# Adding transfers of a gated attention and gMLP block, moved from the vs stage and the first u pair to the pairs of keys, values and queries

## Chip, cores and metric

The kernel runs on one core of a Trainium2 chip, in one launch. The metric is the device time of an execution in microseconds (us). An engine is named as in the profile: PE (TensorE matmuls), DVE (VectorE), ACT (ScalarE), POOL (GpSimd) and SP (SyncE). POOL and SP each feed a DMA queue; ACT's is hardly used.

## What is computed

One layer over 1024 positions of width 1024, in float32. All weights of the input projection are one matrix `w_in`, whose columns are split among q, k, v, za, u, vs, zs and the merge gates.

```python
h = rmsnorm(x, norm_g[l])
q, k, v, za, u, vs, zs, gm = jnp.split(h @ w_in[l], IN_SPLITS, axis=-1)
q, k = partial_rope(q), partial_rope(k)
a = window_sink_attention(q, k, v, att_sinks[l])
a = (a * silu(za)) @ w_att_out[l]
sgo = chunked_spatial_gating(gelu(u), gelu(vs), sg_w[l], sg_b[l], sg_ln_g[l], sg_ln_b[l])
sgo = (sgo * silu(zs)) @ w_sg_out[l]
ga, gs = jnp.split(sigmoid(gm + b_merge[l]), 2, axis=-1)
x = x + (ga * a + gs * sgo) @ w_o[l]
return rmsnorm(x, final_g)
```

`chunked_spatial_gating` normalises vs over its 1024 columns and mixes it over 128 positions with a masked matrix of each channel group; the result is multiplied by u.

## The kernel before

**Split products.** Every float32 factor is split into a high and a low part of TensorE's rounded float32 type: ACT casts the high part, DVE subtracts it for the low one (`split`, lines 188 and 189). A product then takes three matmuls (high by high, high by low, low by high).

**Pairs and seven products.** The large products are made a pair of 128-column blocks of weights at a time (`gemm_pair`), by Strassen's scheme (in Winograd's form): seven products of 128 by 512 by 512 in place of eight. One product is 12 matmuls of 128x512 (`product`, line 399). The scheme needs four sums of each weight pair's quarters. For some pairs (u, keys and values, q and others: `pair_job`) DVE makes them from the loaded tiles `wr` (lines 291 to 295); the first sum needs the second loaded tile of the pair, r1. For the others (`early_job`) they are made in DRAM, long before their use, by **adding transfers**: six DMA steps for each pair, which POOL issues (line 351): two plain copies (512 KB each) and four transfers that add 256 KB to what is there. The list `early` holds 88 steps: six steps each of twelve pairs of weights, and 16 of `w_o` (line 534). They are taken from the front of the list, one at a time, by `part_of_early`, which is called at hooks in the program. Outside the attention stage 44 steps at most may be taken (`keep_of_early`); the rest go beside attention.

**Pacing.** A step is not free to go as soon as POOL reaches it: `paced` makes it wait for the instruction in `pace[0]`. While `by_products[0]` is set, that is a matmul in the middle of the latest product (`product`, at k equal to 1), otherwise a copy by ACT (`mark`). POOL takes its instructions in order, so everything behind a step in POOL's order waits too.

**Stages.** In order: the norm of x; the vs stage (`vs_gemm`, `plain`, `take`), written out by hand in its order; four pairs of u; one pair of keys and values; four pairs of q; two of zs; then attention beside eight pairs of gates, in a written order; then the rest of zs, za, the two output projections, `w_o` and the last norm. Outside the written parts a scheduler at build time sets each engine's order; the order of PE's instructions in all of these pairs is that of the code.

**A pair in time.** In `gemm_pair` ACT copies the first product out of its PSUM bank (x11, line 433), negates the second (x22, line 440) and copies the third's sum (x12, line 443), and DVE adds the later products to these (lines 448, 455, 459). The third product goes on into the bank that x11 is copied from, so that it can't begin before that copy. Four times in a pair `split_next` splits a tile of weights for what comes next; the loads of the pair after next start when its three buffers `wr` come free. A hook is called seven times in a pair, after each product's part.

In the u pairs the hook also mixes: PE multiplies the normalised vs by the mixing matrix into a bank `ps_tp` (line 1126), of which there are two; DVE scales it (line 1134) and multiplies u by it (line 1142), which frees the bank; SP stores the result. Ahead of the first mixing DVE normalises vs (line 1090).

In the pair of keys and values POOL issues the stores of k (`k_dr`, line 1189) and, after a transposition, of v (`v_dr`, line 1204). Their tiles lie in a pool that the q stage's tiles reuse: the first tiles `qhl` (line 1256 on ACT) and `rot` (line 1276 on POOL, and the load of the rotary tables by SP, line 1231) wait until all those stores have landed. A q pair writes each of its four results as a split tile `qhl` (three buffers), which SP stores (`q_hl`, line 1261).

Of the kernel before, what the change touches and what calls it, by code (L numbers as in the profile page):

```python
# [54 lines left out]
def hybrid_tile(  # L55
# [40 lines left out]
    def bank(tag, dt=F32):  # L96
        return pools.get(tag, psum).tile([P, 512], dt, name=nm("ps_" + tag), tag="ps_" + tag, bufs=2)
# [10 lines left out]
    def xtile():  # L108
        return mtile([P, HALF], F32, "x", 5)
# [98 lines left out]
    def new_b(names=FORMS):  # L208
        return {n: (slot(n + "h"), slot(n + "l")) for n in names}
# [38 lines left out]
    def split_next(hold=False):  # L248

        if not units:  # L250
            begin_job()
        if not units:
            return
        halves, keys = units.pop(0)
        if keys[0][1] == 2 and not locked[0]:
            make_sums(behind_of.get(keys[0][0]))
        if callable(halves):
            halves = halves()
        hi = mtile([P, D], F32R, "wh", 3)
        lo = mtile([P, D], F32R, "wl", 3)  # L260
        if isinstance(halves, list):
            for c, half in enumerate(halves):
                split(hi[:, half_of(c)], lo[:, half_of(c)], half)
        else:
            wide = halves.shape[1]
            if hold:
                nc.scalar.copy(hi[:, 0:wide], halves)
                for c, key in enumerate(keys):
                    ready[key] = hi[:, half_of(c)], lo[:, half_of(c)]
                return lambda: nc.vector.tensor_sub(lo[:, 0:wide], halves, hi[:, 0:wide].bitcast(F32))  # L270
            first = split(hi[:, 0:wide], lo[:, 0:wide], halves)
            splits.append(first)
            if keys[0] == (done[0] - 1, 6) and done[0] > LAST_OF_Q + 2 and not locked[0]:
                make_sums(first)
        for c, key in enumerate(keys):
            ready[key] = hi[:, half_of(c)], lo[:, half_of(c)]
        if len(units) == 1 and not locked[0]:
            begin_job()

    def half_of(half):  # L280
        return slice(half * HALF, (half + 1) * HALF)
# [109 lines left out]
    done = [0]  # L391
# [17 lines left out]
    by_products = [False]  # L409

    def product(acc, part, form, fresh, cols=slice(0, HALF)):
        for k in range(4):
            mm = quarter(acc, part, form, k, fresh, cols)
            if k == 1 and by_products[0]:
                pace[0] = mm

    def mark(copy):
        if not by_products[0]:
            pace[0] = copy

    def gemm_pair(b, finish, hook=lambda: None, second="o", begun=None, last_form=None):

        n = done[0]
        done[0] += 1
        if begun:
            acc = begun.pop(0)
        else:
            acc = bank("mm")[:]  # L430
            product(acc, ready[n, 0], b["b11"], True)
        x11, x12, x22 = xtile(), xtile(), xtile()
        mark(nc.scalar.copy(x11[:], acc))
        hook()
        if begun:
            t5 = begun.pop(0)
        else:
            t5 = bank("o")[:]
            product(t5, ready[n, 2], b["t1"], True)
        mark(nc.scalar.mul(x22[:], t5, -1.0))  # L440
        hook()
        product(acc, ready[n, 3], b["t2"], False)
        mark(nc.scalar.copy(x12[:], acc))
        split_next()
        hook()
        t2 = bank(second)[:]
        product(t2, ready[n, 1], b["b21"], True)
        term[0] = nc.vector.tensor_add(x11[:], x11[:], t2)
        finish(0, 0, x11, x11[:], 1.0)
        split_next()  # L450
        if last_form:
            last_form()
        hook()
        product(acc, ready[n, 4], b["t3"], False)
        term[0] = nc.vector.tensor_sub(x22[:], x22[:], acc)
        finish(1, 1, x22, x22[:], 1.0)
        hook()
        product(t5, ready[n, 5], b["b22"], False)
        term[0] = nc.vector.tensor_add(x12[:], x12[:], t5)
        finish(0, 1, x12, x12[:], 1.0)  # L460
        split_next()
        hook()
        product(acc, ready[n, 6], b["t4"], False)
        finish(1, 0, xtile(), acc, -1.0)
        split_next()
        hook()
# [74 lines left out]
    def part_of_early(every=2):  # L541
        hooks[0] += 1
        if len(early) <= keep_of_early and not locked[0]:
            return
        if early and hooks[0] % every == 0:
            early.pop(0)()
# [4 lines left out]
    def put(dst, m, half, src, queue=nc.sync):  # L551
        queue.dma_start(place(dst, m, half), src)
# [77 lines left out]
    hb = new_b(("b11", "b21"))  # L630
# [5 lines left out]
    def tokens(t):  # L636
        return slice((t % 4) * P, (t % 4 + 1) * P)
# [57 lines left out]
    def step_of(acc, hi, lo, wh, wl, first, last):  # L695
        for n, (lt, rt) in enumerate(((hi, wh), (hi, wl), (lo, wh))):
            mm = nc.tensor.matmul(  # L697
                acc, lt, rt, start=first and n == 0, stop=last and n == 2, skip_group_check=True
            )
        return mm  # L700
# [232 lines left out]
    def take(name, c, done=None):  # L933

        s = NAMES.index(name)
        into = t5s if name in ("t1", "b22") else vs_acc
        wh, wl = weights[4 + 2 * s + c]
        hi, lo = hb[name]
        for p in (1, 2, 3):
            for k in range(2):  # L940
                at = 2 * c + k
                pace[0] = step_of(
                    into[p],
                    hi[:, at, tokens(p)],
                    lo[:, at, tokens(p)],
                    wh[:, half_of(k)],
                    wl[:, half_of(k)],
                    name == "t1" and at == 0,
                    at == 3,
                )  # L950
            if c:
                done(p, into[p], xh[:, p + 4, 0:HALF], xh[:, p + 4, HALF:D])
            if (s > 1 and p != 2 + c % 2) or (s == 1 and c and p < 3):
                part_of_early(1)

    def negative(p, acc, q1, q2):
# [23 lines left out]
    with tc.manual_schedule(engines={mybir.EngineType.PE, mybir.EngineType.Activation, mybir.EngineType.DVE}):  # L980
# [36 lines left out]
        of_raw()  # L1017
        form("t3", f12, (1,))
        take("t2", 0)
        of_raw()  # L1020
        take("t2", 1, plus)
# [43 lines left out]
    def hook():  # L1065
        if len(late) > 1 or last_u[0]:
            for _ in range(2):
                if late:
                    late.pop(0)()
# [73 lines left out]
        put(s1_dr, g, half, q[:])  # L1143

    def both():
        part_of_early(1)
        hook()

    by_products[0] = True
# [2 lines left out]
    for m in range(0, KC, 2):  # L1152
        last_u[0] = m == KC - 2

        def finish(i, half, q, src, sign, m=m):
            nc.scalar.activation(q[:], src, AF.Gelu, scale=sign)
            late.append(lambda: mix(m + i, half, q))

        late.append(lambda m=m: bias.append(bias_of(m // 2)))
        gemm_pair(hb, finish, both)  # L1160
    by_products[0] = False
    while late:
        late.pop(0)()
    stage.close()
# [48 lines left out]
            nc.scalar.mul(q[:], src, sign)  # L1213
        (values_of if i else keys_of)(half, q)

    gemm_pair(hb, finish, hook)
    stage.close()


# [31 lines left out]
    def split_q(src, places, keep=False):  # L1251

        hl = mtile([P, 2, HALF], F32R, "qhl", 3, pool)
        hi, lo = (hl[:, a, :].rearrange("p (t q c) -> p t c q", c=2, q=64) for a in range(2))
        src = src.rearrange("p (t c q) -> p t c q", c=2, q=64)
        nc.scalar.mul(hi, src, SC)
        for c in range(2):
            nc.vector.scalar_tensor_tensor(
                lo[:, :, c], src[:, :, c], SC, hi[:, :, c].bitcast(F32), op0=ALU.mult, op1=ALU.subtract
            )  # L1260
        stores = [lambda at=at, dst=dst: nc.sync.dma_start(dst, hl[at].bitcast(F32)) for at, dst in places]
        if keep:
            kept.extend(stores)
            return
        for store in stores:
            store()
# [79 lines left out]

    steps_of_q = []

    def part_of_q():
        while steps_of_q:  # L1350
            if next(steps_of_q[0], 0) is None:
                return
            steps_of_q.pop(0)

    for m in range(0, KC, 2):

        def finish(i, half, q, src, sign):
            if sign < 0:
                nc.scalar.mul(q[:], src, sign)
            put(q_raw, m + i, half, q[:])  # L1360
            rows = slice((m + i) * P, (m + i + 1) * P)
            split_q(q[:], [(slice(0, P), q_hl[:, rows, half_of(half)].rearrange("a p t -> p a t"))])

        if m == 2:
            steps_of_q.append(rope_tables())
        if m == 4:
            steps_of_q.append(rotate_keys(0))
            steps_of_q.append(rotate(0, 3))
        gemm_pair(hb, finish, part_of_q)


    steps = [(g, t, par) for g in range(2) for t in range(NT) for par in range(2)]
# [446 lines left out]
    with tc.manual_schedule(engines={mybir.EngineType.PE, mybir.EngineType.Activation, mybir.EngineType.DVE}):  # L1819
        p = 0  # L1820
# [510 lines left out]
```

## Time and profile before

| | us |
|---|---|
| median of three runs | 899.78 |
| lowest and highest | 896.85, 899.86 |
| the profiled execution | 897.1 |
| its span, first to last instruction | 895.3 |
| PE busy | 883.6 |
| DVE busy | 702.5 |
| ACT busy | 560.0 |
| POOL busy | 163.3 |

The page names the chain of work that ended last; the trace answers for a stretch of time what each engine did, in us from the span's start, and what ended the idle time before an instruction (in square brackets). "SPq" is SP issuing a DMA. Matmuls overlap one another: each shows 0.39 us, and one begins every 0.23 us. By the start times of their products the first u pair runs from about 97 to 119 us, the pair of keys and values from 191 to 211, and the four q pairs from there to about 288.

### The profile page before, as it was taken

What the parts mean: (1) busy time and instruction counts of PE and PEld (TensorE: products, weight loads), DVE (VectorE), ACT (ScalarE), POOL (GpSimd) and SP (SyncE); (2) the same over time, 40 slices, a digit from 0 to 9 for tenths busy, and PEclk for the clock granted to TensorE, in tenths of its full rate; (3) what the DMA queues carried; (4) which work ended last, traced back from release to release, by engine and by line L of the source; (5) the groups of instructions that cost most, each with busy time, mean ns of one, the idle gap of its engine ahead of it and who ended that gap; (6) DMA issues with size and microseconds to landing.
All of it is one profiled execution on the core that took longest, in us unless ns stands there. A gap on an engine that the chain in (4) does not pass through costs nothing.

```text
span 895.3 us, 13284 instructions
## 1 busy us (share of the span) xinstructions
PE 883.6 (99%) x4141; PEld 733.0 (82%) x4141; DVE 702.5 (78%) x1356; ACT 560.0 (63%) x1094; POOL 163.3 (18%) x267
## 2 busy tenths in 40 slices
PE   8999999999999999999999999999999999999997
PEld 5888878888888888888888888888888888888885
DVE  7978856675678669888888887665798699579986
ACT  7777833334445558889888896443575385467543
POOL 4113222213021012222211211111001111110013
PEclk9999999999999999999999999999999999999999
DMA  8699999867788989999998995875559566998533
GB/s 286 170 225 218 281 199 182 172 144 230 242 276 261 284 248 323 300 283 275 273 357 247 273 281 148 304 267 175 176 184 342 193 202 179 295 325 283 191 118 118
DMA packets 131541, 213.32 MB, mean 238 GB/s; under 512 B 13100, under 2 KB 60848, under 8 KB 131472
## 3 DMA queue, kind: packets, MB, share of 16 engines
q1 hardware_dynamic: 108648, 148.89, 51.7%
q0 software_dynamic: 22672, 63.45, 30.0%
q8 instruction: 33, 0.54, 0.2%
q14 instruction: 36, 0.29, 0.1%
q10 hardware_dynamic: 152, 0.14, 0.0%
HBM read 155.68 MB, written 90.31 MB: 275 GB/s over the span
## 4 chain that ended last, share of the span: by engine, by line
PE 93%; DMA 4%; DVE 2%; ACT 0%; SPq 0%; issue 0%; DVEq 0%; ACTq 0%
PE ps_mm L399 44%; PE ps_o L399 26%; PE ps_tp L399 4%; PE ps_sc L399 2%; PE ps_two L1496 2%; PE ps_sc L697 2%; PE ps_mm L697 2%; DMA wr<-in_w_dram 2%; PE ps_o L697 2%; PE ps_tp L1571 2%; PE ps_o L1633 2%; DMA wT<-in_sg_w_dram 1%; PE ps_tp L1126 1%; PE ps_tp L697 1%; PE ps_o L1641 1%; PE ps_tp L1583 1%
## 5 line engine op out<-in xcount | busy, mean ns | idle before, releaser
L189 DVE TENSOR_TENSOR wl<-wr,wh 128x512 fp32r<-128x512 f32 (+1 forms) x65 | 61.8, 953 | 69.8 <-ACT wh L188 69.6
L188 ACT CAST wh<-s 128x1024 fp32r<-128x1024 f32 (+1 forms) x68 | 67.9, 1000 | 77.8 <-issue 22.1
L188 ACT CAST wh<-wr 128x512 fp32r<-128x512 f32 (+1 forms) x65 | 54.0, 832 | 62.3 <-PE ps_mm L399 36.1
L189 DVE TENSOR_TENSOR wl<-s,wh 128x1024 fp32r<-128x1024 f32 (+1 forms) x68 | 78.9, 1160 | 11.4 <-ACT wh L188 11.2
L351 POOL DMA_DIRECT2D sums<-in_w_dram x48 | 34.7, 724 | 145.3 <-PE ps_mm L399 89.4
L399 PE MATMUL ps_o<-T_t1h,wh 128*128 128x512 f32 x148 | 58.4, 395 | 0.0
L399 PE MATMUL ps_o<-T_b22h,wh 128*128 128x512 f32 x148 | 57.9, 391 | 0.0
L399 PE MATMUL ps_o<-T_t1h,wl 128*128 128x512 f32 x148 | 57.8, 391 | 0.0
L399 PE MATMUL ps_o<-T_b22h,wl 128*128 128x512 f32 x148 | 57.8, 390 | 0.0
L399 PE MATMUL ps_o<-T_b22l,wh 128*128 128x512 f32 x148 | 57.8, 390 | 0.0
L399 PE MATMUL ps_o<-T_t1l,wh 128*128 128x512 f32 x148 | 57.7, 390 | 0.0
L1543 ACT ACTIVATE pr<-pr,sm 128x193 f32<-128x193 f32 (+2 forms) x128 | 55.9, 439 | 2.3 <-DVE sm L1527 1.5
L399 PE MATMUL ps_mm<-T_t4h,wh 128*128 128x512 f32 (+1 forms) x144 | 56.4, 391 | 0.0
L399 PE MATMUL ps_mm<-T_t3h,wh 128*128 128x512 f32 x140 | 55.5, 396 | 0.0
L399 PE MATMUL ps_mm<-T_t4h,wl 128*128 128x512 f32 (+1 forms) x144 | 55.5, 385 | 0.0
L399 PE MATMUL ps_mm<-T_t4l,wh 128*128 128x512 f32 (+1 forms) x144 | 55.5, 385 | 0.0
L399 PE MATMUL ps_mm<-T_b11h,wh 128*128 128x512 f32 x140 | 54.8, 392 | 0.0
L399 PE MATMUL ps_mm<-T_t3h,wl 128*128 128x512 f32 x140 | 54.7, 391 | 0.0
L399 PE MATMUL ps_mm<-T_b11l,wh 128*128 128x512 f32 x140 | 54.6, 390 | 0.0
L399 PE MATMUL ps_mm<-T_t3l,wh 128*128 128x512 f32 x140 | 54.6, 390 | 0.0
L399 PE MATMUL ps_mm<-T_b11h,wl 128*128 128x512 f32 x140 | 54.6, 390 | 0.0
L399 PE MATMUL ps_mm<-T_t2h,wl 128*128 128x512 f32 x140 | 54.6, 390 | 0.0
(499 smaller groups left out, 2531.5 us busy)
## 6 DMA issues: line engine op xcount, KB each, us to landing
wr<-in_w_dram SPq DMA_DIRECT2D x80, 256.0 KB
sums<-in_w_dram POOLq DMA_DIRECT2D x24, 512.0 KB, 9.8
s<-sums SPq DMA_DIRECT2D x24, 512.0 KB
wr<-in_w_dram SPq DMA_DIRECT2D x17, 512.0 KB
q_hl<-qhl SPq DMA_DIRECT2D x16, 512.0 KB
q<-q_hl SPq DMA_DIRECT2D x64, 128.0 KB
y_dr<-x POOLq DMA_DIRECT2D x28, 256.0 KB, 6.4
sums<-in_w_dram POOLq DMA_DIRECT2D x24, 256.0 KB, 7.6
```

The lines of the kernel that those rows point to most:

```text
L188: hi_casts.append(nc.scalar.copy(hi, src))
L189: return nc.vector.tensor_sub(lo, src, hi.bitcast(F32))
L351: return lambda: paced(nc.gpsimd.dma_start(dst, src, accum_op=op))
L399: mm = nc.tensor.matmul(acc, lt, rt, start=fresh and k == 0 and n == 0, stop=k == 3 and n == 2, skip_group_check=True,)
L697: mm = nc.tensor.matmul(acc, lt, rt, start=first and n == 0, stop=last and n == 2, skip_group_check=True)
L1126: nc.tensor.matmul(pm[:, t * P : (t + 1) * P], xh[:, half * 4 + t, g * P : (g + 1) * P], bias[-1][1][:, g % 2, :], start=True, stop=True,)
L1496: nc.tensor.matmul(st.sc[:, i], q_of[:, c, i * P : (i + 1) * P], kt[:, :, lo:hi], start=True, stop=True)
L1543: nc.scalar.activation(v, v, AF.Exp, bias=st.nmax[:, c, i : i + 1], scale=-1.0, accum_out=st.sums[:, c, i : i + 1])
L1571: nc.tensor.transpose(st.inner[0 : P if st.t else 64, at : at + P], st.pr[:, i, place_of(c, 64 if st.t else P, 192)], ident[:],)
L1583: nc.tensor.transpose(st.ends[0:wide, i * P : (i + 1) * P], st.pr[:, i, 129 : 129 + wide], ident[:])
L1633: nc.tensor.matmul(st.po[:], lt, rt, start=i == 0, stop=False, skip_group_check=True)
L1641: nc.tensor.matmul(st.po[:, cols(c)], ends[:, c, vs], st.b[:, cols(c)], start=False, stop=c == 1, skip_group_check=True)
```

## The change

Steps are taken at other places, one for one; no step is added or taken away, and nothing is computed otherwise.

- In vs, `take` takes a step only in its last three products and for one of three tiles: 6 steps instead of 14.
- In the first u pair none is taken (`done[0]` is 1 there); the other three take 7 each as before: 21 instead of 28.
- The pair of keys and values calls `both` as its hook: 7 steps, where there were none.
- The q pairs call `beside_q`, which takes a step at every second call until 44 have been taken in all: 10 steps, the last in the third q pair.
- `by_products[0]` is cleared after the q pairs and not after u, so these steps are paced by matmuls.
- Beside attention there are 44 steps left instead of 46.

```diff
-            if (s > 1 and p != 2 + c % 2) or (s == 1 and c and p < 3):
+            if s > 1 and p == 1:
                 part_of_early(1)
...
     def both():
-        part_of_early(1)
+        if done[0] > 1:
+            part_of_early(1)
         hook()
...
         gemm_pair(hb, finish, both)
-    by_products[0] = False
...
-    gemm_pair(hb, finish, hook)
+    gemm_pair(hb, finish, both)
...
+    def beside_q():
+        part_of_early(2)
+        part_of_q()
+
...
-        gemm_pair(hb, finish, part_of_q)
+        gemm_pair(hb, finish, beside_q)
+    by_products[0] = False
```

PE's order is the same in both. On the others the scheduler's order follows the moved steps at a few places.

On POOL, around the pair of keys and values: `sums` are the steps, `khl` and `vt` the split tiles of k and v on their way to `k_dr` and `v_dr`. Before:

```order
L351 DMA sums_111<-sums_111 128x512
L351 DMA sums_112<-sums_112 128x512
L1189 DMA k_dr<-khl_1878 64x2x512 x4
L1203 COPY vt_1907<-vt_1907 128x8x64
L1189 DMA k_dr<-khl_1927 64x2x512
L1204 DMA v_dr<-vt_1907 128x4x384
L1189 DMA k_dr<-khl_1927 64x2x512 x3
L1203 COPY vt_1977<-vt_1977 128x8x64
L1204 DMA v_dr<-vt_1977 128x4x384
L1276 MEMSET rot_2341 128x512
L1276 MEMSET rot_2342 128x512
```

And now, from the last step ahead of the first k store (the steps ahead of it are those of u and of the pair's first products):

```order
L351 DMA sums_109<-sums_109 128x512
L1189 DMA k_dr<-khl_1866 64x2x512 x4
L1203 COPY vt_1897<-vt_1897 128x8x64
L1189 DMA k_dr<-khl_1917 64x2x512
L1204 DMA v_dr<-vt_1897 128x4x384
L1189 DMA k_dr<-khl_1917 64x2x512 x3
L351 DMA sums_110<-sums_110 128x512
L351 DMA sums_111<-sums_111 128x512
L1203 COPY vt_1969<-vt_1969 128x8x64
L351 DMA sums_112<-sums_112 128x512
L1204 DMA v_dr<-vt_1969 128x4x384
L351 DMA sums_106<-sums_106 128x512
```

Three steps now stand between the last store of k and the second store of v, and three more between that and the clearing of `rot`.

On ACT, from the first q pair into the second: `wh` is a split tile of weights, `x<-ps_mm` the last result of the first pair, and L433 the copy x11 of the second pair. Before:

```order
L1256 ACTIVATE qhl_2052<-x_2002 128x4x2x64
L1256 ACTIVATE qhl_2075<-x_2004 128x4x2x64
L188 CAST wh_2105<-s_2099 128x1024
L1256 ACTIVATE qhl_2094<-x_2003 128x4x2x64
L188 CAST wh_2129<-s_2102 128x1024
L1359 ACTIVATE x_2121<-ps_mm_1989 128x512
L1256 ACTIVATE qhl_2124<-x_2121 128x4x2x64
L433 COPY x_2156<-ps_mm_2143 128x512
```

And now:

```order
L188 CAST wh_2099<-s_2093 128x1024
L1256 ACTIVATE qhl_2045<-x_1994 128x4x2x64
L1256 ACTIVATE qhl_2069<-x_1996 128x4x2x64
L1256 ACTIVATE qhl_2088<-x_1995 128x4x2x64
L188 CAST wh_2124<-s_2096 128x1024
L1363 ACTIVATE x_2116<-ps_mm_1981 128x512
L433 COPY x_2151<-ps_mm_2138 128x512
L1256 ACTIVATE qhl_2119<-x_2116 128x4x2x64
```

The first `qhl` stands behind one more cast of weights, and the copy x11 ahead of the fourth `qhl`. The copy x11 and the `qhl` before it change places in the same way from the fourth q pair into the first zs pair.

## The prediction, before the run

> **What bounds the kernel now.** First the page, for the shares of the engines.
>
> ```profile
> span 895.3 us, 13284 instructions
> PE 883.6 (99%) x4141; PEld 733.0 (82%) x4141; DVE 702.5 (78%) x1356; ACT 560.0 (63%) x1094; POOL 163.3 (18%) x267
> ```
>
> PE is idle for 895.3 - 883.6 = 11.7 us in all. A change that moves DMA steps can only win what PE loses by waiting for data, so the second view is the list of PE's waits, which is complete with five rows (us in total, times, longest).
>
> ```profile
> PE ps_tp L1126 <- DVE x L1142: 1.9, 1, 1.9
> PE ps_o L610 <- DVE T_b22l L117: 1.5, 1, 1.5
> PE ps_mm L791 <- ACT T_t2h L715: 1.0, 1, 1.0
> PE ps_tp L1571 <- issue: 0.2, 1, 0.2
> PE ps_o L674 <- DVE wr L669: 0.2, 1, 0.2
> ```
>
> Lines 610, 674 and 791 are the kernel's first matmuls, before any step; line 1571 is attention. One wait is left that the moved steps can touch: a mixing of the u pairs (line 1126). PE's timeline has it at the end of the first u pair.
>
> ```profile
> 121.36 0.39 PE L399 MATMUL ps_mm<-T_b11h,wl 128*128 128x512 f32 x1
> 123.69 1.13 PE L1126 MATMUL ps_tp<-wT,xh 128*128 128x128 f32 x8 [1.94 <-DVE x L1142]
> ```
>
> Between the two starts lie 2.33 us, where 0.23 is usual: the stall costs 2.10 us. DVE's timeline says why the multiplication by u (line 1142), which frees the bank, was late.
>
> ```profile
> 108.34 0.69 DVE L189 TENSOR_TENSOR wl<-wr,wh 128x512 fp32r<-128x512 f32 x1
> 113.39 0.68 DVE L455 TENSOR_TENSOR x<-x,ps_mm 128x512 f32<-128x512 f32 x1
> 117.33 0.69 DVE L294 TENSOR_TENSOR s<-wr 128x512 f32<-128x512 f32 x1 [3.26 <-DMA wr<-in_w_dram]
> 122.86 1.27 DVE L1142 TENSOR_TENSOR x<-x,ps_tp 128x512 f32<-128x512 f32 x2
> ```
>
> DVE stood still for 3.26 us before the first sum of the second u pair (line 294), and line 1142 stands behind it in DVE's order. That sum needs r1, whose two loads SP issued as soon as line 189 had freed the buffer, at 108.34 + 0.69 = 109.03:
>
> ```profile
> 109.05 1.02 SPq L240 DMA_DIRECT2D wr<-in_w_dram  x2
> ```
>
> They had landed at about 117.3: 8.2 us for 512 KB. So the chain is a DMA, then DVE, then PE.
>
> **What each part removes and adds.** The sum is made against the profiled execution, 897.1 us, whose span is 895.3 (1.8 us lie around it). The median of the runs is 2.7 us above it; I take the same difference off both.
>
> *The steps taken out of vs and the first u pair.* How crowded the DMA was there is seen in the issues of POOL (steps, KB each, median us to landing), for 85 to 97 us, 98 to 119 us and 146 to 190 us:
>
> ```profile
> sums<-in_w_dram POOLq DMA_DIRECT2D x7, 512.0 KB, 13.6
> ...
> sums<-in_w_dram POOLq DMA_DIRECT2D x7, 256.0 KB, 12.2
> ...
> sums<-sums POOLq DMA_DIRECT2D x14, 256.0 KB, 6.0
> ```
>
> A step of 256 KB took 12.2 us in the first u pair and 6.0 later, at the same distance between steps: the pair inherits the backlog of vs. Now vs has 6 steps over three products instead of 14, and the pair none. How soon r1 lands without them no row shows; the nearest is the rate of the very first stretch, where only loads run (share of the 16 DMA engines and GB/s are the last two columns).
>
> ```profile
> 5.00:15.00 10.00, 8.64 (x40) 5.66 (x40) 8.55 (x18) 6.99 (x13) 6.08 (x4) 1.00 1.02 405
> 145.00:191.00 46.00, 46.00 (x238) 39.13 (x237) 30.30 (x47) 15.02 (x23) 11.37 (x14) 1.00 0.90 176
> 191.10:211.30 20.20, 20.20 (x92) 16.50 (x92) 12.38 (x19) 7.20 (x11) 3.29 (x6) 1.00 0.59 151
> 211.30:269.00 57.70, 57.70 (x262) 47.65 (x261) 39.95 (x70) 26.41 (x39) 10.13 (x17) 1.00 0.79 260
> ```
>
> At 405 GB/s 512 KB are 1.3 us; the bounds are 1.3 and the present 8.2. PE's stall is gone if line 294 starts 2.1 us sooner, so if r1 lands within 6.1 us. I take that as met, since 6.1 is nearly five times the bare transfer. If r1 lands at once, DVE starts line 294 at 113.39 + 0.68 = 114.07, and the first multiplication of line 1142 ends at about 123.5 - 3.26 = 120.2, 1.4 us before PE asks for it at 121.6; what is late next is nothing. **-2.1 us**, between 0 and -2.1.
>
> *The other three u pairs* keep seven steps each, but now the 512 KB copies fall into them. The cover is DVE's spare time in the second pair (r1's loads, the sum that needs them, and PE's next use of the mixing banks):
>
> ```profile
> 131.70 0.81 SPq L240 DMA_DIRECT2D wr<-in_w_dram  x2
> 139.82 0.69 DVE L294 TENSOR_TENSOR s<-wr 128x512 f32<-128x512 f32 x1
> 156.21 0.89 PE ps_tp L1126 x8
> ```
>
> The sum starts 8.1 us after the issue without a wait, and DVE's last multiplication there ends near 148.5, 7.7 us before PE's next mixing. Even a load as slow as the 13.6 us above is covered: **0**; with the cover gone, a us for each us beyond 7.7.
>
> *The clearing of the fourth `wT`* (line 1097) now stands behind three steps of the second u pair on POOL, and SP's load of `wT` waits for it, with the s1 stores and the weights of 131.70 queued behind it.
>
> ```profile
> 124.88 0.20 POOL L1097 MEMSET wT<- 64x128 f32 x1 [3.38 <-PE ps_tp L1126]
> 170.74 0.24 PE ps_sc L1112 x2
> ```
>
> The third step is paced by the middle of the third product, about 126 us, so it moves by 2 us; weights are asked for 6.8 us and the tile is used 45 us after 124.88. **0.**
>
> *The 7 steps beside keys and values and 10 beside three q pairs.* Their price on the 16 engines is bounded by the window rows. Below: the 14 steps of 145 to 191 us raised the share from 0.59 (the pair of keys and values, without steps) to 0.90, so 0.31 x 46 / 14 = 1.0 us each. Above: they came every 46 / 14 = 3.3 us and their landing time stayed at 6.0, so at most 3.3 each. Stores of the same size on the same queue give a value between:
>
> ```profile
> 205.31 2.47 POOL L1189 DMA_DIRECT2D k_dr<-khl  x4 [15.40 <-DVE khl L189]
> 218.72 0.77 POOL L1204 DMA_DIRECT2D v_dr<-vt  x1 [3.55 <-issue]
> 223.19 1.00 POOL L1276 MEMSET rot<- 128x512 f32 x2 [3.69 <-DMA v_dr<-vt]
> ```
>
> Eight k stores of 256 KB and two v stores of 768 KB, 14 units of 256 KB, went from 205.31 to 223.19: 1.3 us a unit. I take 1.3. The q pairs then go from 0.79 to 0.79 + 10 x 1.3 / 57.7 = 1.02, between 0.96 and 1.36: full, hardly over. A pair's weights are loaded a pair ahead, and that covers waits of some us on them: **0**, with the price in the rivals.
>
> *The second v store* is the sharpest place: three steps stand ahead of it, and a fourth is still under way when the k stores begin. It landed at 223.2; now at 223.2 + 4 x 1.3 = 228.4, between 227.2 and 236.4. ACT's first `qhl` waits for it, and behind that stand, in ACT's new order, two more `qhl`, a cast, the pair's last result and the copy x11 (line 433):
>
> ```profile
> 223.16 0.69 ACT L1256 ACTIVATE qhl<-x 128x512 fp32r<-128x512 f32 x1
> 230.21 1.05 ACT L188 CAST wh<-s 128x1024 fp32r<-128x1024 f32 x1 [1.15 <-PE ps_mm L399]
> 231.17 0.59 ACT L1359 ACTIVATE x<-ps_mm 128x512 f32<-128x512 f32 x1
> 233.10 0.59 ACT L433 COPY x<-ps_mm 128x512 f32<-128x512 f32 x1 [0.63 <-PE ps_mm L399]
> ...
> 235.62 0.39 PE L399 MATMUL ps_mm<-T_t2h,wh 128*128 128x512 f32 x1
> ```
>
> Together 3 x 0.69 + 1.05 + 0.59 + 0.59 = 4.3 us, and the third product at 235.62 needs the copy: the store may land as late as 231.3. At 228.4 there are 2.9 us left: **0**, between 0 and +5.1. SP's rotary tables and `q_hl` stores wait for the same landing and follow within that margin.
>
> *ACT's order into the first zs pair.* There x11 was held up by a `qhl` that waited for its buffer, and the third product begins at 293.84 (its row in the chain):
>
> ```profile
> 292.44 0.67 ACT L1256 ACTIVATE qhl<-x 128x512 fp32r<-128x512 f32 x1 [2.66 <-DMA q_hl<-qhl]
> 293.00 0.57 ACT L433 COPY x<-ps_mm 128x512 f32<-128x512 f32 x1
> 293.84 2.80 PE ps_mm L399 x12
> ```
>
> 0.27 us were left; with x11 first this wait no longer threatens PE. Nothing is won, since nothing was lost. The two steps fewer beside attention change nothing either: PE waits 0.2 us there in all.
>
> Sum: -2.1 us. The profiled execution would take 895.0, its span 893.2; the median 899.8 - 2.1 = **897.7 us**. A measurement of this kernel can tell about 0.5% from no change, 4.5 us, so the forecast is "no change".
>
> **Rivals.** *The v store takes the stall's place.* If a step costs more than 2.0 us in POOL's queue, four of them bring the store past 231.3, and PE waits in the second q pair: up to 5.1 us, 2 in the middle. For it: 3.3 us is not excluded. Against: 1.3 for stores. Time 899.7, between 898 and 902.8.
>
> *The DMA is overfull in the q pairs, and the kernel becomes slower.* Each pair hides 2.7 us of lateness, the time of the product between the one that x11 copies and the one that needs the copy. At 3.0 us a step there are 0.79 x 57.7 + 30 - 57.7 = 17.9 us of transfers too many, 8.1 of them hidden in three pairs: +9.8, so 907.5. It is slower by more than 4.5 from 14.7 us on, 2.7 us a step. For it: the 2.66 us wait on a `q_hl` store above, at 0.86 of the engines or so. Against: the price is twice that of a store, and half of these transfers would have to meet a wait.
>
> *r1 stays late.* If the two queues take turns at the DMA engines, a backlog on POOL's can cost SP's load no more than as much again as the load itself: 1.3 us of 512 KB at 405 GB/s. Line 294 then starts 1.3 us sooner and 0.8 us of the stall stays: 898.5. For it: 8.2 us is much more than 2.6, so something other than the share would be in it. Against: steps' landing times halved where the backlog was gone. The Trainium skill (DMA: Bandwidth & Descriptors, "Queues, rings and completion order") states such a rule: each DMA engine goes round the queue rows that have work, a packet of one before the next. By that rule the change wins 1.3 us here and not 2.1; that a step's landing time grows with its own queue's backlog fits it, while how the load's time was shared no row shows.
>
> *The same stall is longer in the other runs.* They lie 2.7 us above the profiled one; PE has little else that can vary. Then 4.8 us go: 895.0, faster by 0.53%. Nothing shown places the spread.
>
> **How the numbers follow.** Forecast 0.50, v store 0.19, r1 late 0.13, spread 0.12, overfull 0.06. The first three are within 0.5%: 0.82; faster 0.12; slower 0.06. The range goes from 894.5, half a us below the fourth, to 902.0, into the upper part of the v store's; left out are the overfull case, the last of the v store's and some scatter, near 2 in 10.
>
> **What would show it.** Right: PE's waits without the row of line 1126 at 2 us, no DMA wait over 1.2 us before line 294 in the first u pair, PE's products 2.72 us apart from there to 290 us, the clearing of `rot` released by a v store before 231. Wrong: a row of PE waiting for ACT's line 433 or 1256, or for DVE's line 448, between 210 and 300 us; line 294 still waiting 2 us or more; or a loss of time beside attention, where I see none.

## The result and the profile after

The changed kernel takes 907.98 us (median of 6 executions, 906.39 to 908.56), the kernel before 898.34 (6 executions beside them): a ratio of 1.0107, with a 95% interval of 1.0087 to 1.0126. It is slower; I had forecast no change, 897.7, with a range up to 902.0. Ratios here and below lie close to those of the means, so that a ratio isn't always the quotient of the two medians.

The page after, two lines:

```profile
span 904.4 us, 13283 instructions
PE 886.4 (98%) x4141; PEld 733.2 (81%) x4141; DVE 702.7 (78%) x1356; ACT 558.1 (62%) x1094; POOL 162.8 (18%) x267
```

The span is 9.1 us longer. Each engine has the work that it had within 2 us, but PE is busy 2.8 us longer; it is now idle for 18.0 us in place of 11.7. The first three rows of its waits after (us in total, times, longest):

```profile
PE ps_mm L399 <- ACT x L433: 3.4, 3, 1.5
PE ps_mm L399 <- DVE x L455: 2.9, 2, 2.3
PE ps_mm L399 <- ACT x L443: 1.9, 1, 1.9
```

The row of line 1126, 1.9 us, is gone, as forecast. These three stand in its place, which the list of before didn't have: the products wait for copies and sums of a pair's results. All but 0.6 us of them (at 798 us) lie between 238 and 302 us. They add up: idle time grew by 18.0 - 11.7 = 6.3, which is 3.4 + 2.9 + 1.9 less the 1.9 that went; the other 2.8 us are busy time, 1.5 of it at a halved clock (last section). The windows say what else is new there (PE's busy time first; the last three columns are the granted clock, the share of the DMA engines and GB/s):

```profile
97.00:119.00 22.00, 22.00 (x111) 18.66 (x110) 20.95 (x42) 15.01 (x23) 0.00 (x0) 1.00 0.25 83
119.00:145.00 26.00, 26.00 (x137) 22.20 (x137) 17.09 (x25) 8.97 (x14) 4.55 (x9) 1.00 0.82 241
145.00:191.00 46.00, 46.00 (x237) 39.16 (x236) 30.29 (x49) 15.57 (x23) 11.39 (x14) 1.00 0.94 172
191.10:211.30 20.20, 20.20 (x94) 16.44 (x93) 9.70 (x14) 8.15 (x12) 9.22 (x14) 1.00 1.00 238
211.30:269.00 57.70, 53.27 (x237) 43.11 (x235) 36.12 (x63) 21.96 (x33) 15.79 (x24) 1.00 0.98 254
```

The first u pair has the DMA engines nearly to itself (0.25), and PE doesn't wait up to 211 us. In the pair of keys and values the share went from 0.59 to 1.00, and in the q pairs from 0.79 to 0.98, while the bytes in the q pairs did not rise (260 GB/s before, 254 now). More engine time for no more bytes: something in there is dear. Two queues share that time. The DMA view for 211 to 231 us (packets, MB, share of the 16 engines; q0 is POOL's queue, q1 is SP's), first before:

```profile
q0 software_dynamic: 792, 2.88, 45.7%
q1 hardware_dynamic: 3144, 2.45, 38.2%
```

and after:

```profile
q0 software_dynamic: 1359, 3.68, 79.2%
q1 hardware_dynamic: 2274, 1.42, 25.6%
```

SP's queue, which brings the weights and stores q, moves 1.42 MB where it moved 2.45. How that reaches PE is seen at 255 us, where PE waits 1.46 us for line 433. ACT's timeline:

```profile
255.54 0.66 ACT L1256 ACTIVATE qhl<-x 128x512 fp32r<-128x512 f32 x1 [4.32 <-DMA q_hl<-qhl]
256.10 0.56 ACT L433 COPY x<-ps_mm 128x512 f32<-128x512 f32 x1
```

The copy x11 (line 433) stands in ACT's order behind a `qhl` that waits 4.32 us for one of its three buffers, so for a store of q to land; the third product needs x11. In total ACT waited for these stores, before and after:

```profile
ACT qhl L1256 <- DMA q_hl<-qhl: 3.5, 4, 2.7
```

```profile
ACT qhl L1256 <- DMA q_hl<-qhl: 23.9, 5, 7.7
```

The longest wait, 2.28 us, comes another way: through the weights. DVE's and PE's timelines and SP's issues after:

```profile
251.88 3.44 SPq L240 DMA_DIRECT2D wr<-in_w_dram  x3
...
262.10 0.69 DVE L294 TENSOR_TENSOR s<-wr 128x512 f32<-128x512 f32 x1 [4.51 <-DMA q_hl<-qhl]
...
269.45 0.68 DVE L455 TENSOR_TENSOR x<-x,ps_mm 128x512 f32<-128x512 f32 x1
...
270.18 0.50 PE L399 MATMUL ps_mm<-T_t4h,wh 128*128 128x512 f32 x1 [2.28 <-DVE x L455]
```

DVE stood still for 4.51 us before the first sum of the fourth q pair's weights. The profile puts this down to a store of q; in the program the sum waits only for the four loads of that pair's second tile (r1). Three of them were issued from 251.88 to 255.32, and the last landed at about 262; before, they were issued from 248.72 to 250.69, and the sum began at 253.75 without a wait. From 262.10 on DVE worked without a pause, with line 455 behind its backlog. Of the 4.51 us some 2.2 were covered, and 2.28 reached PE.

The stores are late because SP issues them late and because they take long. The chain of waits after, with pieces left out:

```profile
222.46 10.83 DMA wr<-in_w_dram
...
233.30 0.61 SPq L1398
...
234.66 4.63 DMA q_hl<-qhl
...
249.22 6.24 DMA q_hl<-qhl
```

A load of 128 KB of weights takes 10.83 us, and a load of v (line 1398), which needs no weights, is issued when it has landed. The program says why; in SP's order, with the places in it and the semaphore that each waits for:

```
100 L240 DMA wr_2129<-in_w_dram 128x2x128 [waits DMAHW6_49]
108 L1398 DMA v_3085<-v_dr 64x2x192 [waits DMAHW6_49]
```

SP's transfers count their landing on eight semaphores in turn, and each waits for the one that had its semaphore eight places earlier. So eight at most are under way, and when they take longer SP issues less often. The first q store, behind these, was issued at 234.02; before, at 227.83, and in e1_no_bytes below, with the same order on SP, at 227.37. That the eight places hold it up is read from the program and the chain; no run took them away.

### The profile page after: what moved, and what is told of

Read it like the earlier page. It is cut to its first block, busy times and chain, and to the rows that moved or that the text cites. A ratio compares the mean times of both kernels' runs of the same rounds, so it can differ in the third digit from the quotient of the medians.

```text
span 904.4 us, 13283 instructions
## 1 busy us (share of the span) xinstructions
PE 886.4 (98%) x4141; PEld 733.2 (81%) x4141; DVE 702.7 (78%) x1356; ACT 558.1 (62%) x1094; POOL 162.8 (18%) x267
## 3 DMA queue, kind: packets, MB, share of 16 engines
q0 software_dynamic: 22672, 63.45, 29.6%
## 4 chain that ended last, share of the span: by engine, by line
PE 87%; DMA 7%; DVE 2%; issue 1%; ACT 1%; SPq 1%; DVEq 0%; ACTq 0%
PE ps_mm L399 40%; PE ps_o L399 23%; PE ps_tp L399 4%; DMA wr<-in_w_dram 3%; DMA q_hl<-qhl 3%; PE ps_mm L697 2%; PE ps_o L697 2%; PE ps_sc L399 2%; PE ps_two L1501 2%; PE ps_sc L697 2%; PE ps_tp L1126 2%; PE ps_tp L1576 2%; PE ps_o L1638 2%; PE ps_tp L697 1%; DMA q_raw<-x 1%
## 5 line engine op out<-in xcount | busy, mean ns | idle before, releaser
L399 PE MATMUL ps_mm<-T_t2h,wh 128*128 128x512 f32 x140 | 54.9, 392 | 3.4 <-ACT x L433 3.4
L399 PE MATMUL ps_o<-T_b22l,wh 128*128 128x512 f32 x148 | 57.7, 390 | 0.0
L399 PE MATMUL ps_o<-T_t1l,wh 128*128 128x512 f32 x148 | 57.7, 390 | 0.0
```

What stands on the lines that cost most here:

```text
L399: mm = nc.tensor.matmul(acc, lt, rt, start=fresh and k == 0 and n == 0, stop=k == 3 and n == 2, skip_group_check=True,)
```

## The experiments

What was to be told apart: **bytes** (the steps' transfers beside keys, values and queries take DMA time that SP's transfers need), **order** (on SP the rotary tables and two v loads now stand ahead of the first four q stores), and which of the two places does it. All twelve ran beside the kernel before, whose median was 895.3 to 895.7 us there.

| run | us | ratio to before (95%) |
|---|---|---|
| e1_no_bytes | 898.21 | 1.0038 (1.0019 to 1.0056) |
| e2_kv_only | 905.58 | 1.0112 (1.0092 to 1.0132) |
| e3_q_only | 909.51 | 1.0151 (1.0123 to 1.0178) |
| e4_thin | 900.26 | 1.0051 (1.0031 to 1.0071) |
| e5_u1_to_kv | 894.49 | 0.9998 (0.9986 to 1.0010) |
| e6_plain | 902.75 | 1.0092 (1.0073 to 1.0111) |
| e7_before_again | 895.30 | 1.0001 (0.9987 to 1.0015) |
| e8_x11_first | 905.98 | 1.0118 (1.0102 to 1.0134) |
| e9_after_again | 909.01 | 1.0141 (1.0120 to 1.0161) |
| e10_five | 900.18 | 1.0045 (1.0030 to 1.0061) |
| e11_packets | 911.03 | 1.0165 (1.0136 to 1.0195) |
| e12_ten | 906.50 | 1.0119 (1.0090 to 1.0149) |

**The changed kernel without the bytes.**

```diff
-            return lambda: paced(nc.gpsimd.dma_start(dst, src, accum_op=op))
+            rows = lambda: slice(0, 1 if small[0] and op == ALU.add else P)
+            return lambda: paced(nc.gpsimd.dma_start(dst[rows()], src[rows()], accum_op=op))
...
+    small[0] = True
     gemm_pair(hb, finish, both)
```

> The changed kernel, every engine's order as it is, but the 15 adding steps that are taken beside keys, values and queries add one row of 128 and not all (the other two steps there are plain copies and stay whole), so that nearly nothing is moved by them. This leaves most of those sums unmade. If the loss comes from the bytes that the steps move through the DMA engines beside keys, values and queries, the time falls from 908 to what I forecast for the change, 895 to 899, the stalls of PE between 230 and 310 us go, and the first four q_hl stores land before 235. If it comes from the order on SP, where the rotary tables and two v loads now stand ahead of the first q_hl stores, or from POOL's pacing of the k and v stores, it stays at 904 to 908, with the 2.0 us stall at 238.6.

898.21. Of PE's waits between 190 and 315 us one row is left (line numbers are a few higher in some of these kernels):

```profile
PE ps_mm L401 <- DVE x L457: 0.2, 1, 0.2
```

The page's row of POOL's queue, first of the changed kernel and then of this one, gives a step's price:

```profile
q0 software_dynamic: 22672, 63.45, 29.6%
```

```profile
q0 software_dynamic: 20992, 59.55, 26.8%
```

29.6% of 904.4 us are 267.7 us of all 16 engines, 26.8% of this run's 895.0 are 239.9: the 15 adding steps took 27.8, so 1.86 us each (an estimate by difference: it takes the queue's other transfers as equal in both). Every engine's order is that of the changed kernel here, SP's with it, so order is out as the main cause. 0.38% is left; a wait of 0.9 us for the sum of line 455 near 788 us, also in the changed kernel (0.6 us), is part of it. The rest I can't place.

**Which of the two places.** The steps that are not taken go beside attention, whose last three pairs then take one at every product.

```diff
-    keep_of_early = len(early) - 44
+    keep_of_early = len(early) - 34
...
-                    part_of_early(1 if p < 5 else 2)
+                    part_of_early(1)
```

> Of the 17 moved steps only the 7 beside keys and values are taken there; the 10 of the q pairs go beside attention (its last three pairs take a step at every product). On SP the tables and one v load still stand ahead of the first q_hl stores. If the bytes do it, the backlog of 7 steps is worked off in the first q pair: 897 to 901, with no stall after 245 us. If SP's order does it: 902 to 906, with the stall at 238.6 kept.

905.58, but neither theory's way: no wait of PE between 190 and 315 us, and a long one in attention, where the ten steps went (`ps_two` are attention's scores). Its own list of waits, and its window of the second q pair:

```profile
PE ps_two L1501 <- DMA q<-q_hl: 6.3, 2, 5.9
```

```profile
231.00:250.00 19.00, 19.00 (x89) 15.74 (x89) 13.45 (x30) 9.23 (x14) 0.00 (x0) 1.00 0.78 273
```

So the seven steps beside keys and values are worked off in the first q pair, and the end of attention has no room for ten more. (Here and in e4_thin two of the twelve made sums are loaded ahead of their last addition, so that their values differ; what that does to the time was not tested.)

```diff
-    gemm_pair(hb, finish, both)
+    gemm_pair(hb, finish, hook)
...
-    keep_of_early = len(early) - 44
+    keep_of_early = len(early) - 37
```

> Only the 10 steps beside the q pairs are taken; the 7 beside keys and values go beside attention. SP's order there is almost that of the kernel before: the first four q_hl stores come ahead of the second rotary table and the v loads. If the bytes do it, 901 to 906: the stalls at 255, 267 and 300 us stay in part and the one at 238.6 goes. If SP's order does it, 895 to 899, no stall.

909.51: worse than either theory had it. The ten beside the q pairs alone make the whole of it, on an SP order in which the first four q stores come early (the first is issued at 227.79). All ten add here; in the changed kernel eight of its ten do, and two are copies of 512 KB:

```profile
PE ps_mm L399 <- ACT x L433: 6.7, 2, 4.0
PE ps_mm L399 <- DVE x L455: 0.9, 1, 0.9
```

(Attention adds some 3 us in this run. The clock is halved for some 13 us of it, behind the longest waits, against 3 us in the changed kernel; that is part of why it is slower.)

> vs and the first u pair as in the changed kernel, but none of the steps beside keys, values or queries: five more go beside u pairs 2 to 4 and the rest beside attention. Every theory that puts the loss into the keys, values and q pairs has 895 to 898 here, 2.1 us under the kernel before, with the wait of PE for line 1142 gone and none in its place. Over 900 would say that fewer steps early cost time in themselves, or that attention has no room for ten more.

900.26, above what all theories said; the q pairs have no wait, and attention again pays for its ten more (1.8 us at one place), with 1.1 us near 790. As a clean measure of the thinning it fails.

**One move alone, and the kernel before once more.** The kernel before, with `if done[0] > 1` in `both` and the pair of keys and values calling `both`; vs, q and attention stay.

> The kernel before with one move alone: the 7 steps of the first u pair are taken beside keys and values; vs keeps its 14, the q pairs have none, attention its 46. What the runs so far say (the 7 steps beside keys and values cost no stall in the q pairs, the 10 beside q cost over 10 us) gives the time of the kernel before or up to 2 us less, with no stall of PE between 190 and 310 us. If the 7 steps beside keys and values were part of the loss, 899 to 903. If vs's 8 steps were what made r1 late, the wait of PE for line 1142 stays.

> The kernel before, once more, for its profile on this chip, where its time was 895.5 in the last runs and not 899. If the 2.1 us wait of PE for line 1142 is what varies between chips and runs, it is missing or under 0.5 us here and the span is about 893; if it stands, the difference lies somewhere else.

894.49 and 895.30. PE's whole list of waits with the one move, and the row at stake in the kernel before on this chip:

```profile
PE ps_o L610 <- DVE T_b22l L117: 1.5, 1, 1.5
PE ps_mm L791 <- ACT T_t2h L715: 1.0, 1, 1.0
PE ps_o L674 <- DVE wr L669: 0.2, 1, 0.2
PE ps_sc L618 <- DVE wh L604: 0.2, 1, 0.2
```

```profile
PE ps_tp L1126 <- DVE x L1142: 1.0, 1, 1.0
```

The move takes the stall away and brings none. But the stall was 1.0 us here where it had been 1.9, and the kernel's span was no shorter for it (895.6 against 895.3; 892.7 with the move): other waits of the kernel before vary as much. The gain is within the interval, at most 0.14%.

**What of a step is dear.** In the first, the steps beside q that add copy instead; in the second they add, in packets of 512 B.

```diff
-            return lambda: paced(nc.gpsimd.dma_start(dst, src, accum_op=op))
+            return lambda: paced(nc.gpsimd.dma_start(dst, src, accum_op=ALU.bypass if as_copy[0] else op))
...
+    as_copy[0] = True
```

> The changed kernel, every engine's order as it is, but the steps beside the q pairs copy and do not add; the same bytes are written, and the sums come out otherwise. If what costs is that a step adds (it must also read what it adds to), a copy of 256 KB is little dearer than a store: 899 to 902, stalls at 255 and 267 us under 1 us. If what costs is the number of 2 KB packets on POOL's queue beside SP's small ones, nothing changes: 905 to 908.

```diff
-            return lambda: paced(nc.gpsimd.dma_start(dst, src, accum_op=op))
+            return lambda: paced(nc.gpsimd.dma_start(dst, src, accum_op=op, **(small if op == ALU.add else {})))
...
+    small['max_dma_last_dim'] = HALF
```

> The changed kernel, every engine's order as it is, but the steps beside the q pairs that add move their 256 KB in packets of 512 B and not of 2 KB. If SP's small packets wait because POOL's queue holds each engine for a whole large packet in turn, smaller ones give SP its turn sooner: 899 to 903, and POOL's queue has under 60% of the engines' time at 211 to 231 us as far as q steps are in it. If it is the work of the steps as such, four times as many packets cost more: 908 to 915.

> The changed kernel once more, beside the next three. If what is lost beside the q pairs is the same in every execution, it is 10 to 12 us above the kernel before here too (905 to 907 against 895), and the stalls stand at the same places in its profile.

Copies: 902.75, between the two forecasts; adds: 909.01; adds in small packets: 911.03, as the second theory had it. The adds are the changed kernel once more: 2 us slower than expected, with its stalls at the same places (241, 270, 282 and 302 us) but for the one at 255. The DMA view for 211 to 269 us, the rows of POOL's queue and of its 256 KB steps (the last number is their median time to land), of the changed kernel, of the copies, and of the small packets:

```profile
q0 software_dynamic: 2239, 5.17, 46.4%
...
sums<-sums POOLq DMA_DIRECT2D x10, 256.0 KB, 7.6
```

```profile
q0 software_dynamic: 1978, 5.83, 38.5%
...
sums<-sums POOLq DMA_DIRECT2D x10, 256.0 KB, 5.6
```

```profile
q0 software_dynamic: 5281, 5.22, 54.2%
...
sums<-sums POOLq DMA_DIRECT2D x10, 256.0 KB, 9.5
```

Two of these ten steps are still those of keys and values, which add in all three. The seven issued from 218 to 260 us, all beside q, alone: 5.0 us to landing as copies, 7.4 as adds, 9.1 in small packets. With copies more bytes take less of the engines. The waits between 190 and 315 us go from 7.6 us to 3.1 (one row, line 433's). How much of the time the adding itself is, is less certain: beyond e1_no_bytes the copies lose 0.54%, the changed kernel 0.69% by its first ratio (1.0107, whose interval overlaps that of the copies) and 1.03% by its second (1.0141, clear of it). So it is between a fifth and a half. That SP's small packets only wait for large ones to pass finds no support: with smaller ones POOL's queue holds the engines longer, and the run is not faster. As both change at once, it isn't refuted either.

**How much is too much.** The kernel before with 5 or 10 of attention's steps beside the first three q pairs (up to 47 or 52 steps may be taken outside attention, where the kernel before takes 42, and `part_of_early(4)` or `(2)` is called in the hook).

> The kernel before with 5 of attention's steps taken beside the first three q pairs, at every fourth product; vs, u, keys and values as before. If the DMA engines lose in proportion to what is put on them, half of the ten steps' loss: 900 to 902. If each pair hides what it can (2.7 us, the time of a product) and only the rest shows, 5 steps of about 1.9 us each in 58 us are hidden whole: 895 to 897.

> The kernel before with 10 of attention's steps taken beside the first three q pairs, at every second product; vs, u, keys and values as before. If these ten alone make the loss, 905 to 909, the stalls between 230 and 310 us as in the changed kernel and in the run with the q steps only. If the 7 beside keys and values are half of it after all, 899 to 902.

What I had overlooked: attention's first steps are plain copies of 512 KB, so these are doses of copies. Five cost 0.45%, though by the mean of a pair the engines were not full. Windows with five:

```profile
211.00:231.00 20.00, 20.00 (x89) 16.53 (x89) 11.76 (x18) 7.80 (x11) 4.07 (x7) 1.00 0.90 283
231.00:250.00 19.00, 17.42 (x81) 14.10 (x80) 13.77 (x29) 8.62 (x13) 1.37 (x2) 1.00 0.84 290
...
229.00:234.00 5.00, 3.75 (x17) 2.78 (x15) 1.78 (x5) 0.84 (x2) 0.00 (x0) 1.00 1.04 389
```

At a mean share of 0.84 PE already loses 1.6 us of 19. The last row says what the mean hides: in the 5 us before that stall ended the engines were full. A q store issued at 226.96 took 6.1 us to land there, and a `qhl` ahead of x11 waited 4.44 us for it. But the same 5 us are as full in the kernel before (1.03), where PE doesn't wait. With ten, 906.50 looks like the whole loss, but isn't the same one. Two rows of its waits:

```profile
PE ps_mm L399 <- ACT x L433: 4.1, 3, 1.6
PE ps_tp L1126 <- DVE x L1142: 2.0, 1, 2.0
```

Only the first lies in the q pairs, where the changed kernel has 7.6. Ten copies of 512 KB do less harm there than ten adds of 256 KB did in e3_q_only (7.6 as well). The second is the old stall of the first u pair, with a halved clock behind it (last section). Attention adds waits of 1.9 and 1.4 us. Why attention lost 3.3 us in this run, with ten steps fewer, I don't know.

**Is it only ACT's order?** `qhl` of a pair's last result is ordered behind the next pair's x11.

```diff
-        nc.scalar.mul(hi, src, SC)
+        by = nc.scalar.mul(hi, src, SC)
+        if first is not None:
+            after(by, first)
```

> The changed kernel with ACT's order changed at two places: in the third and fourth q pair the copy x11 (line 433) stands ahead of the last qhl of the pair before (line 1256), and no longer behind it. The transfers are the same. If PE loses its time there only because the copy stands behind an instruction that waits for a q_hl store, the stalls at 254.9 and 279.9 go and nothing takes their place: 904 to 906. If the late transfers find another way (weights for the sums, the next copy behind the next qhl), the time is the same within 1 us: 907 to 909.

905.98, a ratio of 1.0118; the changed kernel had 1.0107 and 1.0141. The time lies in the range of the first theory, the waits follow the second. The stall at 254.9 is gone and the one at 279.9 falls to 0.2 us, but the one at 270 grows from 2.3 to 3.9 us and one of 0.5 comes at 286:

```profile
PE ps_mm L400 <- DVE x L457: 3.9, 1, 3.9
PE ps_mm L400 <- ACT x L445: 2.4, 2, 1.9
PE ps_mm L400 <- ACT x L434: 1.0, 2, 0.8
```

7.3 us against 7.6. The wait of 3.9 us is the way through the weights again: DVE stood still for 7.95 us before the first sum of the fourth q pair, which in the program waits for the loads of r1 alone. The span is 0.5 us shorter. The cause is the late transfers, not where ACT meets them.

## Why the prediction was wrong

- **The stall of the first u pair**: right. DVE's timeline after has the sum and the multiplications without a wait:

```profile
112.53 0.68 DVE L294 TENSOR_TENSOR s<-wr 128x512 f32<-128x512 f32 x1
...
118.04 1.27 DVE L1142 TENSOR_TENSOR x<-x,ps_tp 128x512 f32<-128x512 f32 x2
```

  The load of r1 was issued at 108.20, so it landed within 4.3 us, under the 6.1 needed; the rival in which r1 stays late is out. The size was one profile's: in the median the move of the first u pair's steps is worth about 1 us (e5_u1_to_kv).
- **The other u pairs, the clearing of `wT`, and the seven steps beside keys and values**: right. PE is busy throughout 119 to 211 us, and e2_kv_only and e5_u1_to_kv have no loss in the q pairs.
- **The second v store**: right that it costs nothing; it came earlier than forecast (228.4). ACT's first `qhl` after:

```profile
226.65 1.78 ACT L1256 ACTIVATE qhl<-x 128x512 fp32r<-128x512 f32 x3 [0.83 <-DMA sums<-sums]
```

  The profile names a step; in the program this `qhl` waits for the stores of k and v. The second v store was issued at 217.01 and took 9.4 us.
- **The ten steps beside the q pairs: here it failed**, at "a pair's weights are loaded a pair ahead, and that covers waits of some us on them: 0". The load on the engines was forecast well enough: a share of 1.02, and 0.98 came. The price was low, 1.3 us a step against 1.86, because I took it from stores that do not add, though my bounds held it. But neither made the error: I never compared the cover with how late a single transfer may be. It failed in two places. The weights had cover, but only some 2.2 us of it where their sum waited 4.51 us; 2.28 us of that reached PE, and the halved clock behind it took 1.5 more. And I looked at the weights alone. The stores of q had no cover: `qhl` has three buffers for four results a pair, and ACT's in-order queue puts the next pair's copy behind the fourth. A buffer comes back only when its store has landed; the stores in the chain took 3.2 to 6.2 us from the issue, and the first issue itself was 6.2 us late. The other 5.2 us of PE's waits up to 302 us come this way (at 281 us by way of a `qhl` of keys; the profile names another store there, the program a store of q).
- **Threshold**: I let a pair hide 2.7 us and counted as loss what exceeds full engines. By that rule 1.86 us a step would have cost nothing (0.79 x 57.7 + 18.6 - 57.7 = 6.5 us too many, 8.1 hidden). e10_five lost 0.45% at mean shares of 0.84 to 0.90. A mean of 20 us is the wrong measure: it holds stretches at 1.04, and each wait is paid where it falls.
- **The overfull rival**, at 907.5, named the place and nearly the time (907.98), but by a price of 3.0 us that a step doesn't have and by a rule that fails; that its time fits is luck. I gave it 0.06 because I asked whether the engines would be full, and not how late a single store may be.
- **ACT's order into the first zs pair**: wrong that it no longer threatens PE. x11 still stood behind a `qhl` that waited 3.65 us, and PE waited there a little before 302 us.

What I had named as proof against me, PE waiting for line 433 between 210 and 300 us, is the row that came.

## What to carry to other kernels

Before moving background transfers beside a stage, list that stage's stores and loads with the fewest buffers, and ask of each how late it may land and what stands behind it in its engine's order; a mean share of the DMA engines under 1 does not answer that. Price a transfer by its kind: in this kernel one that adds cost the engines more than a copy of its size. Seven steps are free beside the pair of keys and values (share 0.59, slack in the next pair), while ten beside q, and even five copies there, are not: the place decides more than the number.

## What the runs showed of the hardware

**Adding transfers.** Beside the q pairs (218 to 260 us, median of seven) 256 KB took 7.4 us to land as an add and 5.0 us as a copy, DRAM to DRAM both, on the same queue and in the same program order. With packets of 512 B in place of 2 KB the add took 9.1.

**The granted clock.** After the longest wait of PE in the changed kernel (2.28 us, until 270.18) the clock was halved for 3 us. Two windows of the changed kernel, up to 274.6 us and after that:

```profile
271.50:274.60 3.10, 3.10 (x9) 2.38 (x8) 1.91 (x3) 0.31 (x1) 0.00 (x0) 0.50 0.96 322
274.90:278.00 3.10, 3.10 (x15) 2.59 (x14) 0.00 (x0) 0.37 (x1) 0.00 (x0) 1.00 1.04 376
```

At 0.50 those 3.1 us did half their work: 1.5 us more on top of the wait. In e12_ten a wait of 1.99 us, until 123.64, was enough:

```profile
125.50:127.20 1.70, 1.70 (x6) 1.41 (x6) 1.70 (x4) 0.41 (x1) 0.16 (x1) 0.50 0.94 293
```

Over these runs, waits of 1.99 us (e12_ten), 2.23 (e3_q_only) and 2.28 (the changed kernel), and those from 2.76 to 5.87 (e2_kv_only, e3_q_only, e8_x11_first, e9_after_again) came with a halved clock, during them or within 1.5 us of their end. Waits of 1.94 us (the kernel before), 2.03, 2.27 and 2.52 (e11_packets) and 2.48 (e6_plain) did not. So between 2.0 and 2.5 us it isn't the length alone. The Trainium skill (TensorE: Matmul & The Clock Gate, "Part 1: The HAM clock gate") says that activity is judged in windows of about 3.4 us that run freely; whether a wait falls into one window or across two might then decide; that would fit these rows, but none shows where a window begins. It asks for an idle window of that length before the clock is halved; here 1.99 us of waiting did it, and the measurement stands.
